# A one-core transformer layer step: another order for the last norm and the last gate, and other sources for some low halves of weights

## The chip, the core and the metric

The kernel runs on one core of one Trainium2 chip. A core has TensorE (matmuls; "PE" in the profile, "PEld" its weight loads), VectorE (DVE), ScalarE (ACT), GpSimd (POOL) and SyncE (SP), which here only issues transfers. Each engine works off its own queue in order. The metric is the device time of one execution in microseconds; three runs of the kernel before gave a median of 2521.23 us (2519.8 to 2523.84).

## The reference

One layer is applied to 2048 prompt tokens (empty states) and to 64 tokens of a second sequence (given states), with a model width of 1024:

```python
h = rms_norm(x, g_pre)
vA, bA, cA, zA, q, f, iv, zB, gA, gB = split_cols(h @ w_in)            # ten blocks of 1024 columns
u = cA * vA
yA = (silu(zA) * bA * causal_conv3(u_ext, conv_w)) @ w_a_out
fg = lb + (1 - lb) * sigmoid(f); logf = log(fg); kk = 1 - fg; qq = silu(q) * QK_SCALE
S_new, o = hgrn2_scan(S0, qq, kk, iv, logf)                            # 8 heads, chunks of 64 tokens
o = o * rsqrt(mean(o * o) + EPS) * g_onorm
yB = (o * silu(zB)) @ w_b_out
out = (sigmoid(gA) * yA + sigmoid(gB) * yB) @ w_o
x = x + rms_norm(out, g_post)
gate = sigmoid(rms_norm(x, g_ple) @ w_ple_gate)                        # "the last gate"
x = x + (p @ w_ple_proj) * gate
```

Results are x for both sequences and the new convolution and scan states.

## The kernel before, in words

**Number format.** Everything is float32. TensorE gets each weight and each operand as two parts: the high half, a cast that ScalarE writes, and the low half, the raw value minus the high half, a subtraction of VectorE. Both stand on line L230 (`split`). Each product takes three matmuls: high by high, high by low, low by high.

**Columns.** The 2112 tokens are worked off in three blocks of 768, 704 and 640 columns, features on the partitions. A block has two halves; a matmul of the last block has 320 columns. Temporaries (`r`) come from a ring of 48 tiles, half tiles (`hf`) from 8. Weights lie in `raw` (5 buffers), `hi` (4), `lo` (4) and `s` (3).

**Products.** Input projections come in groups of two output blocks (`sgroup`, matmuls on L457 to L459): seven products in place of eight, with sums S1 to S4 of weight blocks, sums T1 to T4 of operand blocks and the weight blocks A11, A12 and A22 themselves. Each product takes one 256 KB weight tile. The output projections (W_A, W_B, W_O) and the last block's W_G, which is the last gate, are done "in turn" (`in_turn`, L608 to L610): product 1 for all four pairs of output blocks, then product 2, and so on. The operand of the next product (for instance T2 = B22 - B12, line L562, and its split) is prepared while the present one runs, one tile after each pair.

**Low halves of weights.** `split_w` either makes a low half with the subtraction on VectorE or loads it from DRAM (`lows`), where block 1 left it: one more transfer of 256 KB on SyncE's queue, no work for VectorE, and a cast on L279 instead of L230 for the high half. Which way a sum goes is decided in `kept_w` by the list `fresh`: sums whose name stands there are subtracted anew. One list holds for the whole program; whoever reads it gets what was last written:

```python
return split_w(load_raw(sums[i1][name]), None if name in fresh else (i1, name), name in fresh)
```

In the last block `fresh` is empty for the gates and for `path_b`, holds S1 and S2 in `path_a`, and is cleared behind it. A12 and A22 of the input projections are always subtracted.

**Stages.** For each block: the gates gA and gB (8 groups; for the second and third block seven of them, `LEAD`, run right after the W_O of the block ahead, and the eighth inside `path_a`, when `side` calls `next(fills)` at j == 2), `path_b` (8 heads; per head one group for f and iv and one for zB and q), `path_a` (8 times two groups), W_A, W_B, W_O, and the norms. The attention of a head is hung between the matmuls of the next head's groups by hooks: scores on L1110, p_u on L1142, p_o on L1180 and L1182, the norm over a head's outputs with its power on GpSimd (L700 and L702) and the scaling on L1199. VectorE's gating of the keys and queries (L978 to L1038) stands between the splits of the same queue.

**End.** After the last block's W_O: its `final_norm` (squares of the eight output tiles on L741, added on L742; TensorE's transposes for the sum over features on L722; power on L702; scaling by g_post on L1446, + x on L1447; second squares; second root; scaling by g_ple on L1469). It is spread over the hooks of the `final_gate` of the block ahead, whose inputs wait in DRAM ("held": loaded by `asked`, split by `held_parts`), and of `ple`, the product p @ w_ple_proj. Then the last gate runs in turn; its `sink` applies the sigmoid (L1518), multiplies (L1520), adds x (L1521) and stores. Tables of numbers in `spread_out` say how many steps of each plan run at each hook.

Of the kernel before, what the change touches and what calls it, by code (L numbers as in the profile page):

```python
# [20 lines left out]
KB = D // P  # L21
# [73 lines left out]
def hybrid_step(  # L95
# [476 lines left out]

    def in_turn(stages, operand):

# [11 lines left out]

        for k in range(2):
            prepare(1, k)
        for i, (st, n) in enumerate(todo):
# [4 lines left out]
            for g in range(KH):  # L594
# [33 lines left out]
                elif what in ("p5", "p7"):  # L628
# [4 lines left out]
                    st["sink"](g, 1, 1, u2, p57)  # L633
                if i > 0:
                    prepare(i + 1, g)
                elif g < KH - 2:
                    prepare(1, g + 2)
# [240 lines left out]
    def gates(bl, hc, kept, first):  # L878


        groups = [(kind, j) for kind in (GA, GB) for j in range(0, KB, 2)]
        for kind, j in groups[: -1 if first else None]:
            outs = [rt(), rt()]
            n = groups.index((kind, j))
            sgroup(kind * 8 + j, kind * 8 + j + 1, hc, gate_sink(outs), first, by_k=n == 0 and not first, anew=n < LEAD)
            keep_gates(kept, kind, j, outs)
            yield
# [531 lines left out]

    def final_norm(bl, xo, acc, kept, take, early):  # L1420

        segs = bl["segs"]
        acc2, xks = None, []

        def fetch():
# [4 lines left out]

        for j in range(KB):
            sum_squares(j, xo[j], acc, width[0])
            if j % 2:
                yield
# [7 lines left out]
        for j in range(KB):  # L1444
            fetch()
            V.scalar_tensor_tensor(xo[j], xo[j], g_post[:, j : j + 1], rs, ALU.mult, ALU.mult)  # L1446
            V.tensor_tensor(xo[j], xo[j], xks[j], ALU.add)  # L1447
            if j == 0:
                acc2 = rt()
            sum_squares(j, xo[j], acc2, width[0])  # L1450
            yield
        stored = iter(range(0 if bl["last"] else KB))

        def store(n):
            for i in islice(stored, n):
                kept["x", i] = spill("x", i)
                paced(G.dma_start(kept["x", i], xo[i]))

        rs2 = rt()
# [35 lines left out]
    def final_gate(bl, h2, kept, by_k=False):  # L1495

        segs = bl["segs"]
        for j in range(KB):
            if by_k and j < 2:
                both = gemm_by_k([W_G, W_G + 1], h2, segs, (1,)) if j == 0 else both  # L1500
                pss = both[j]
            else:
                pss = gemm(W_G + j, h2, segs, (1,) if by_k else ())
            xj, pj, t = reload(kept["x", j]), reload(kept["p", j]), rt()
            for s, ps in zip(segs, pss):
                A.activation(t[:, cols_of(s)], ps, AF.Sigmoid)
            V.tensor_tensor(t, pj, t, ALU.mult)
            V.tensor_tensor(t, t, xj, ALU.add)
            G.dma_start(y_fm[j * P : (j + 1) * P, bl["t0"] : bl["t0"] + bl["n"]], t)
            yield  # L1510

    def gate_in_turn(bl, h2, xs, kept):


        def sink(g, c, h, x, y):
            j, s = g + c * KH, whole(x, y)
            t = hf() if y is None else s
            A.activation(t, s, AF.Sigmoid)  # L1518
            v = half(kept["p", j], h)
            (G if c == h == 0 else V).tensor_tensor(v, v, t, ALU.mult)  # L1520
# [149 lines left out]
    for bi, bl in enumerate(blocks):  # L1670
# [78 lines left out]
        for idx, n in in_turn(stages, a_first):  # L1749
# [3 lines left out]
            elif nxt and (idx, n) == (W_B, 6):  # L1753
                spread_out((next_ops(), (0, 1, 0, 1, 0, 1, 0) * KH))
            elif bl["last"] and idx == W_O and 1 <= n <= 4:
                run(asked, 2)
            elif bl["last"] and (idx, n) == (W_O, 5):
                a_first.clear()
                norm = sized(bl, final_norm(bl, xo, rt(), kept, lambda j, t: h2.append(t), 0))
                spread_out(  # L1760
                    (held_parts, (1,) * 4 + (2, 2)),
                    (norm, (0,) * 4 + (1,) * 4 + (2, 1, 0, 1, 1, 1, 2, 1, 2, 1, 1, 0) + (1, 1, 2, 1, 2, 1, 1)),
                    (sized(bl, ask_p()), (0,) * 16 + (1, 0, 0, 1)),
                    (sized(bl, first_halves()), (0,) * 24 + (1,) * 4),
                )
        if nxt:
            xo.extend(stages[-1]["mid"])
            fills = sized(nxt, gates(nxt, hc, kepts[bi + 1], False))
            norm = sized(bl, final_norm(bl, xo, rt(), kept, partial(split_h, h2) if first else partial(keep_h, kept), int(first)))
            spread_out((norm, (1,) * 6 + (0,) * 5 + (1, 0, 0, 1, 1) + (0, 1) * (KB - 1) + (0, 0, 1, 0, 0, 1) + (1, 0) * (KB - 3) + (1, 1, 1)))  # L1770
# [7 lines left out]
        else:  # L1778
# [55 lines left out]
```

## Time and profile before

| | us |
|---|---|
| median of three runs | 2521.23 |
| the profiled execution | 2522.08 |
| its span | 2520.4 |
| TensorE busy in it | 2495.2 (99%) |
| VectorE busy | 1943.3 (77%) |
| ScalarE busy | 1504.2 (60%) |
| GpSimd busy | 530.9 (21%) |
| DMA, mean over the span | 294 GB/s |

The stages that the change touches lie in the profiled execution about here: the seven groups of the last block's gates at 1690 to 1776 us, its `path_b` up to 2016, its `path_a` with the eighth gate group up to 2224, W_A, W_B and W_O up to 2374, the `final_gate` of the second block up to 2444, `ple` up to 2459, the last gate up to 2514, and the last stores up to 2520. A row of the profile's groups reads: line, engine, operation, output<-input, shapes, count | busy us, mean ns of one | idle time of the engine just before, and who ended most of it. A row of a table of windows reads: the stretch, its length, then for each engine the busy time with the instructions in brackets, then TensorE's granted clock, the share of the DMA engines' time, and GB/s.

### The profile page before, as it was taken

How to read it: one execution, taken by the hardware profiler on the slowest of the kernel's cores; microseconds unless marked ns; L12 is line 12 of the kernel's file. 1: busy time of each engine (PE TensorE's matmuls, PEld its weight loads, DVE VectorE, ACT ScalarE, POOL GpSimd, SP SyncE). 2: the span in 40 equal slices, each digit the busy share in tenths (PEclk: the TensorE clock that was granted, in tenths of full speed). 3: DMA queues.
4: the chain of work that ended last, by engine and by line, in shares of the span. 5: the costliest groups of instructions: out<-in, count | busy, mean ns of one | idle time of the engine just before them, and what ended most of it. 6: DMA issues, size and time to landing. Idle time of an engine off the chain costs nothing. (4 is left out here: it accounts for less than half of the span.)

```text
span 2520.4 us, 47301 instructions
## 1 busy us (share of the span) xinstructions
PE 2495.2 (99%) x16254; PEld 2476.1 (98%) x16254; DVE 1943.3 (77%) x3699; ACT 1504.2 (60%) x2926; POOL 530.9 (21%) x891
## 2 busy tenths in 40 slices
PE   9999999999999999999999999999999999999998
PEld 9999999999999999999999999999999999999998
DVE  7889999988867775588885667977677776679667
ACT  6676676554554763566555555676666655566645
POOL 2032222320022021122223221002122222110133
PEclk9999999999999999999999999999999999999999
DMA  8789889997687798788889988989988879888876
GB/s 330 241 305 338 313 297 324 330 318 266 231 334 263 258 330 292 255 272 284 280 282 332 336 299 310 323 272 355 329 285 290 276 260 324 279 304 307 292 250 212
DMA packets 341937, 741.95 MB, mean 294 GB/s; under 512 B 43062, under 2 KB 48240, under 8 KB 341696
## 3 DMA queue, kind: packets, MB, share of 16 engines
q1 hardware_dynamic: 284832, 515.76, 59.1%
q0 software_dynamic: 56864, 223.16, 24.8%
q8 instruction: 128, 2.10, 0.3%
q14 instruction: 113, 0.93, 0.1%
HBM read 526.40 MB, written 212.36 MB: 293 GB/s over the span
## 5 line engine op out<-in xcount | busy, mean ns | idle before, releaser
L457 PE MATMUL pg<-r,hi 128*128 128x320 f32 (+2 forms) x3304 | 1074.7, 325 | 1.7 <-DVE r L505 1.7
L458 PE MATMUL pg<-r,hi 128*128 128x320 f32 (+2 forms) x3304 | 1066.8, 323 | 0.0
L459 PE MATMUL pg<-r,lo 128*128 128x384 f32 (+2 forms) x2380 | 775.3, 326 | 0.0
L457 PEld LDWEIGHTS pg<-r,hi 128*128 128x128 f32 x3304 | 621.0, 188 | 4.0 <-DVE r L505 2.2
L458 PEld LDWEIGHTS pg<-r,hi 128*128 128x128 f32 x3304 | 621.6, 188 | 0.0
L279 ACT CAST hi<-raw 128x512 fp32r<-128x512 f32 x550 | 339.9, 620 | 407.7 <-PE pg L458 158.8
L459 PEld LDWEIGHTS pg<-r,lo 128*128 128x128 f32 x2380 | 447.1, 188 | 0.3 <-DMA lo<-low 0.3
L230 ACT CAST hi<-raw 128x512 fp32r<-128x512 f32 x420 | 259.4, 621 | 219.8 <-PE pg L458 81.0
L609 PE MATMUL pg<-r,hi 128*128 128x320 f32 (+2 forms) x976 | 313.3, 322 | 1.6 <-DVE r L230 1.5
L608 PE MATMUL pg<-r,hi 128*128 128x320 f32 (+2 forms) x976 | 310.4, 321 | 1.4 <-ACT r L230 1.4
L459 PE MATMUL pg<-r,s 128*128 128x352 f32 (+1 forms) x924 | 291.5, 315 | 2.1 <-DMA s<-low 2.1
L230 DVE TENSOR_TENSOR lo<-raw,hi 128x512 fp32r<-128x512 f32 x320 | 219.4, 687 | 93.5 <-ACT hi L230 88.6
L230 DVE TENSOR_TENSOR r<-r,r 128x320 fp32r<-128x320 f32 (+7 forms) x374 | 221.0, 611 | 44.1 <-ACT r L230 43.3
L230 ACT CAST r<-r 128x320 fp32r<-128x320 f32 (+7 forms) x374 | 195.9, 557 | 34.1 <-DVE r L1353 8.8
L610 PE MATMUL pg<-r,lo 128*128 128x320 f32 (+2 forms) x656 | 209.2, 319 | 0.0
L609 PEld LDWEIGHTS pg<-r,hi 128*128 128x128 f32 x976 | 183.9, 189 | 4.1 <-DVE r L230 3.8
L608 PEld LDWEIGHTS pg<-r,hi 128*128 128x128 f32 x976 | 182.9, 188 | 3.3 <-ACT r L230 2.9
L230 ACT CAST hi<-s 128x512 fp32r<-128x512 f32 x164 | 101.9, 623 | 126.9 <-PE pg L458 99.0
L459 PEld LDWEIGHTS pg<-r,s 128*128 128x128 f32 x924 | 173.5, 188 | 2.4 <-DMA s<-low 2.4
L471 ACT COPY hf<-pg 128x352 f32<-128x352 f32 (+2 forms) x354 | 157.5, 448 | 0.8 <-PE pg L459 0.7
L230 DVE TENSOR_TENSOR lo<-s,hi 128x512 fp32r<-128x512 f32 x164 | 114.1, 696 | 45.0 <-ACT hi L230 40.6
L505 DVE TENSOR_TENSOR r<-hf,pg 128x128 f32<-128x128 f32 (+5 forms) x164 | 64.3, 411 | 95.7 <-PE pg L459 95.4
(391 smaller groups left out, 4239.0 us busy)
## 6 DMA issues: line engine op xcount, KB each, us to landing
raw<-w_blk SPq DMA_DIRECT2D x559, 256.0 KB, 4.5
raw<-S SPq DMA_DIRECT2D x452, 256.0 KB, 4.1
lo<-low SPq DMA_DIRECT2D x332, 256.0 KB, 4.3
s<-low SPq DMA_DIRECT2D x218, 256.0 KB, 4.9
low<-lo SPq DMA_DIRECT2D x207, 256.0 KB, 4.0
S<-s SPq DMA_DIRECT2D x152, 256.0 KB, 4.1
low<-r POOLq DMA_DIRECT2D x66, 256.0 KB, 4.4
r<-w_blk POOLq DMA_DIRECT2D x64, 256.0 KB, 6.6
```

What stands on the lines that cost most here:

```text
L230: return A.copy(hi, src).ins, V.tensor_tensor(lo, src, hi.bitcast(F32), ALU.subtract).ins
L279: A.copy(hi, raw)
L457: add(hi[:, k, :], xhi, start=start and k == 0, stop=False)
L458: add(hi[:, k, :], xlo, start=False, stop=False)
L459: last[0] = add(lo[:, k, :], xhi, start=False, stop=k == KH - 1).ins
L471: copied = A.copy(got[n], ps[bank])
L505: V.tensor_tensor(dst, x, y, ALU.add)
L608: add(hi[:, k, :], xhi, start=start and k == 0, stop=False)
L609: add(hi[:, k, :], xlo, start=False, stop=False)
L610: last[0] = add(lo[:, k, :], xhi, start=False, stop=k == KH - 1).ins
```

## The change

It has six parts.

1. In the gates of the last block, `fresh` is set to S1 to S4 for groups n = 5 and n = 6 and to nothing for other n. It is written only there and, as before, ahead of and behind `path_a`. So it still holds S1 to S4 in all 16 groups of the last block's `path_b`; and it is emptied at j == 2 of `path_a`, where the eighth gate group runs.
2. End phase: the squares of output tiles 4 to 7 go first (before: 0 to 7 in order), and the norm's plan begins one product of W_O earlier. The transposes of the first sum (L722) come two hooks, that is one output block of `final_gate`, earlier, and so does the scaling by g_post. The loads of the held tiles begin one product earlier.
3. The last gate's operands are prepared two products ahead (`lead=2`).
4. The second weight halves of `final_gate` (8 tiles) and A11 and A12 of the last gate (8 tiles) have their low halves loaded.
5. In `final_gate` of the second block the + x (L1508) is done by GpSimd instead of VectorE. In the last gate's sink GpSimd does the multiplications of the first column half, VectorE those of the second; before, GpSimd did only those of output half 0, column half 0.
6. At the end of the second block the stores of x for later (8 of 360 KB on GpSimd's queue) are issued at the scaling of each tile instead of after all of them.

```diff
-    def in_turn(stages, operand):
+    def in_turn(stages, operand, lead=1):
...
-        for k in range(2):
+        for k in range(2 if lead == 1 else KH):
             prepare(1, k)
...
-                if i > 0:
-                    prepare(i + 1, g)
+                if lead > 1 or i > 0:
+                    prepare(i + lead, g)
                 elif g < KH - 2:
                     prepare(1, g + 2)
                 hook()
...
             n = groups.index((kind, j))
+            fresh[:] = ("S1", "S2", "S3", "S4") if bl["last"] and LEAD - 2 <= n < LEAD else ()
             sgroup(kind * 8 + j, kind * 8 + j + 1, hc, gate_sink(outs), first, by_k=n == 0 and not first, anew=n < LEAD)
...
-    def final_norm(bl, xo, acc, kept, take, early):
+    def final_norm(bl, xo, kept, take, early):
...
-        for j in range(KB):
-            sum_squares(j, xo[j], acc, width[0])
-            if j % 2:
+        acc = rt()
+        for i in range(KB):
+            sum_squares(i, xo[(i + KH) % KB if bl["last"] else i], acc, width[0])
+            if i % 2:
                 yield
...
             sum_squares(j, xo[j], acc2, width[0])
+            if not early:
+                store(1)
             yield
...
-                both = gemm_by_k([W_G, W_G + 1], h2, segs, (1,)) if j == 0 else both
+                both = gemm_by_k([W_G, W_G + 1], h2, segs) if j == 0 else both
...
-                pss = gemm(W_G + j, h2, segs, (1,) if by_k else ())
+                pss = gemm(W_G + j, h2, segs)
...
-            V.tensor_tensor(t, t, xj, ALU.add)
+            (G if by_k else V).tensor_tensor(t, t, xj, ALU.add)
...
-            (G if c == h == 0 else V).tensor_tensor(v, v, t, ALU.mult)
+            (V if h else G).tensor_tensor(v, v, t, ALU.mult)
...
-        return dict(idx=W_G, order=IN_TURN, raw=h2, anew=("A11", "A12"), sink=sink)
+        return dict(idx=W_G, order=IN_TURN, raw=h2, anew=(), sink=sink)
...
-            elif bl["last"] and idx == W_O and 1 <= n <= 4:
+            elif bl["last"] and idx == W_O and n < 4:
                 run(asked, 2)
-            elif bl["last"] and (idx, n) == (W_O, 5):
+            elif bl["last"] and (idx, n) == (W_O, 4):
...
-            for idx, n in in_turn([gate_in_turn(bl, h2, xo, kept)], a_first):
+            for idx, n in in_turn([gate_in_turn(bl, h2, xo, kept)], a_first, 2):
```

The built program has 1948 transfers on SyncE's queue instead of 1980: 8 fewer for the two gate groups, 64 fewer in `path_b`, 24 more in `path_a`, 16 more in the end phase.

**VectorE in a head of the last block's `path_b`.** Before, this stretch of its queue runs from the power's first step (L700) through the scaling of the heads' outputs (L1199) to the multiplication on L1026, whose result the scores' matmuls on L1110 read. `raw`, `hi`, `lo`, `s` are the tiles of a weight, `pg` and `pa` banks of matmul results:

```order
L700 TENSOR_SCALAR ms_23895<-ms_23895 128x1
L505 TENSOR_TENSOR r_23739<-hf_23796,hf_23811 128x320
L1199 TENSOR_TENSOR r_23885<-pa_23876,ms_23886 128x512
L1199 TENSOR_TENSOR r_23885<-pa_23892,ms_23895 128x128
L1038 SCALAR_TENSOR_TENSOR r_23740<-pg_23783,vec,r_23740 128x320
L505 TENSOR_TENSOR r_23739<-hf_23796,pg_23798 128x320
L1065 STREAM_TRANSPOSE r_23332<-r_23885 128x5x4x32
L498 TENSOR_TENSOR hf_23942<-hf_23796,pg_23830 128x320
L1025 SCALAR_TENSOR_TENSOR r_23739<-r_23739,r_23949 128x640
L1038 SCALAR_TENSOR_TENSOR r_23740<-hf_23942,vec,r_23740 128x320
L230 TENSOR_TENSOR lo_23990<-raw_23987,hi_23989 128x512
L1026 TENSOR_TENSOR r_23739<-r_23739,r_23727 128x640
```

After (the line numbers are 1 higher here):

```order
L230 TENSOR_TENSOR s_23984<-raw_23981,hi_23983 128x512
L1200 TENSOR_TENSOR r_23885<-pa_23892,ms_23895 128x128
L486 TENSOR_TENSOR hf_23811<-hf_23811,hf_23843 128x320
L498 TENSOR_TENSOR hf_23942<-hf_23796,pg_23830 128x320
L230 TENSOR_TENSOR lo_23990<-raw_23987,hi_23989 128x512
L505 TENSOR_TENSOR r_23739<-hf_23796,hf_23811 128x320
L1039 SCALAR_TENSOR_TENSOR r_23740<-hf_23942,vec,r_23740 128x320
L230 TENSOR_TENSOR s_23996<-raw_23993,hi_23995 128x512
L1066 STREAM_TRANSPOSE r_23332<-r_23885 128x5x4x32
L1026 SCALAR_TENSOR_TENSOR r_23739<-r_23739,r_23949 128x640
L230 TENSOR_TENSOR lo_24002<-raw_23999,hi_24001 128x512
L1027 TENSOR_TENSOR r_23739<-r_23739,r_23727 128x640
```

In a whole head twelve splits of weights (L230) stand on VectorE instead of four, and six more of them stand ahead of L1026 (now L1027).

**VectorE at the last gate's operands.** `hf_31582` and `hf_31613` are T2 for the first two pairs of tiles, made on L562 and then split. Before:

```order
L230 TENSOR_TENSOR lo_31654<-raw_31651,hi_31653 128x512
L562 TENSOR_TENSOR hf_31582<-r_31373,r_31296 128x320
L566 TENSOR_TENSOR r_31373<-r_31373,hf_31582 128x320
L230 TENSOR_TENSOR r_31586<-hf_31582,r_31586 128x320
L562 TENSOR_TENSOR hf_31613<-r_31375,r_31321 128x320
```

After (`hf_31496` is the first T2; L1472 is the scaling by g_ple, L1469 before):

```order
L230 TENSOR_TENSOR r_31375<-r_31296,r_31375 128x320
L559 TENSOR_TENSOR r_31296<-r_31296 128x320
L1472 SCALAR_TENSOR_TENSOR r_31429<-r_28390,vec,r_31191 128x640
L230 TENSOR_TENSOR r_31403<-r_31321,r_31403 128x320
L562 TENSOR_TENSOR hf_31496<-r_31373,r_31296 128x320
L564 TENSOR_TENSOR r_31296<-r_31373,r_31296 128x320
L230 TENSOR_TENSOR r_31431<-r_31346,r_31431 128x320
L1472 SCALAR_TENSOR_TENSOR r_31457<-r_28391,vec,r_31191 128x640
```

The first T2 now stands among the scalings of the norm (L1472) instead of behind them; the tiles of product 2 (B21, the five splits that stand between its L564 and L566 in the queue) and T2 are taken in turn with them.

More of the change, by code (lines that the diff above doesn't have):

```diff
@@ L1418, in out_in_turn, with store @@
         return stage
-    def final_norm(bl, xo, acc, kept, take, early):
+    def final_norm(bl, xo, kept, take, early):
         segs = bl["segs"]
         acc2, xks = None, []
+        stored = iter(range(0 if bl["last"] else KB))
+        def store(n):
+            for i in islice(stored, n):
+                kept["x", i] = spill("x", i)
+                paced(G.dma_start(kept["x", i], xo[i]))
         def fetch():
@@ L1450, in final_norm @@
             sum_squares(j, xo[j], acc2, width[0])
+            if not early:
+                store(1)
             yield
[L1452 to L1457, printed above, removed]
         rs2 = rt()
@@ L1754, in hybrid_step @@
                 spread_out((next_ops(), (0, 1, 0, 1, 0, 1, 0) * KH))
-            elif bl["last"] and idx == W_O and 1 <= n <= 4:
+            elif bl["last"] and idx == W_O and n < 4:
                 run(asked, 2)
-            elif bl["last"] and (idx, n) == (W_O, 5):
+            elif bl["last"] and (idx, n) == (W_O, 4):
                 a_first.clear()
-                norm = sized(bl, final_norm(bl, xo, rt(), kept, lambda j, t: h2.append(t), 0))
+                norm = sized(bl, final_norm(bl, xo, kept, lambda j, t: h2.append(t), 0))
                 spread_out(
[L1761 to L1764, printed above, removed]
+                    (held_parts, (0, 1, 0, 1) + (1,) * 6),
+                    (norm, (0,) * 4 + (0, 0, 1, 1) + (1, 3, 0, 1) + (0, 1, 1, 1, 2, 1, 1, 1, 1, 0, 1, 0) + (1, 1, 1, 2, 1, 1, 1, 1)),
+                    (sized(bl, ask_p()), (0,) * 14 + (1,) + (0,) * 6 + (1,)),
+                    (sized(bl, first_halves()), (0,) * 28 + (1,) * 4),
                 )
@@ L1768, in hybrid_step @@
             fills = sized(nxt, gates(nxt, hc, kepts[bi + 1], False))
-            norm = sized(bl, final_norm(bl, xo, rt(), kept, partial(split_h, h2) if first else partial(keep_h, kept), int(first)))
+            norm = sized(bl, final_norm(bl, xo, kept, partial(split_h, h2) if first else partial(keep_h, kept), int(first)))
             spread_out((norm, (1,) * 6 + (0,) * 5 + (1, 0, 0, 1, 1) + (0, 1) * (KB - 1) + (0, 0, 1, 0, 0, 1) + (1, 0) * (KB - 3) + (1, 1, 1)))
```

## Prediction
> **What bounds the kernel now.** I read the busy times first, then TensorE's waits, then windows over the places that wait, and only then single instructions.
>
> ```profile
> span 2520.4 us, 47301 instructions
> PE 2495.2 (99%) x16254; PEld 2476.1 (98%) x16254; DVE 1943.3 (77%) x3699; ACT 1504.2 (60%) x2926; POOL 530.9 (21%) x891
> ...
> PE pa L722 <- DVE r L742: 3.6, 1, 3.6
> PE pg L459 <- DMA s<-low: 2.1, 1, 2.1
> PE pg L609 <- DVE r L230: 1.5, 3, 0.9
> PE pg L608 <- ACT r L230: 1.4, 2, 0.9
> PE pa L1182 <- DVE r L1157: 1.2, 6, 0.3
> PE pa L1180 <- DVE r L1157: 0.8, 5, 0.2
> PE pa L1110 <- DVE r L1026: 0.5, 1, 0.5
> ```
>
> TensorE is busy for 99% of the span (waits: total us, times, longest). No matmul is removed, so whatever is gained must come from its waits. The last matmul starts here, so 2520.4 - 2513.8 = 6.6 us of tail follow:
>
> ```profile
> 2513.52 0.31 PE L610 MATMUL pg<-r,lo 128*128 128x320 f32 x1
> ```
>
> Two of the waits cost more than they last:
>
> ```profile
> 2434.54:2437.95 3.41, 0.07 (x1) 0.10 (x2) 2.36 (x3) 1.81 (x4) 2.46 (x5) 1.00 1.00 312
> 2437.95:2441.36 3.41, 3.41 (x14) 3.41 (x15) 2.49 (x4) 1.24 (x3) 0.00 (x0) 0.50 0.92 347
> 2475.50:2478.91 3.41, 1.55 (x7) 1.03 (x7) 3.38 (x5) 1.64 (x5) 2.94 (x5) 1.00 0.64 241
> 2478.91:2482.32 3.41, 3.35 (x12) 3.35 (x13) 2.96 (x7) 1.84 (x4) 1.31 (x2) 0.50 0.42 128
> 1768.94:1772.35 3.41, 2.37 (x17) 2.11 (x15) 2.61 (x4) 1.26 (x2) 0.42 (x1) 1.00 1.03 403
> 1772.35:1775.76 3.41, 2.31 (x16) 2.31 (x17) 0.00 (x0) 0.08 (x1) 1.18 (x3) 1.00 1.05 410
> ```
>
> After a stretch of 3.41 us with TensorE busy for 0.07, and after one with 1.55, the next ran at a granted clock of 0.50, which loses half of 3.41 us, 1.7 us, each time. After stretches with 2.37 and 2.31 busy it stayed at 1.00.
>
> **The change part by part.** *Lows of the gates and of `path_b`.* The 2.1 us of L459 lie in gate group n = 6, whose four sum lows are now subtracted: -2.1 us (0 to -2.1; the stores of x move into the same stretch, whose DMA share is 1.03 to 1.05 above). The list is not reset afterwards, so `path_b` of the last block also subtracts S1 to S4: per head eight loads fewer and eight subtractions more on VectorE. One head:
>
> ```profile
> 1880.96:1911.13 30.17, 29.81 (x230) 29.17 (x229) 23.42 (x53) 19.48 (x35) 7.58 (x12) 1.00 0.83 285
> ...
> L978 DVE TENSOR_SCALAR r<-r,lbt 128x640 f32<-128x640 f32 x1 | 0.6, 616 | 2.8 <-ACT r L976 2.8
> L1199 DVE TENSOR_TENSOR r<-pa,ms 128x512 f32<-128x512 f32 x1 | 0.7, 692 | 0.9 <-POOL ms L702 0.9
> L505 DVE TENSOR_TENSOR r<-hf,pg 128x128 f32<-128x128 f32 x2 | 0.5, 284 | 2.2 <-PE pg L459 2.2
> ...
> 1893.45 0.85 DVE L1026 TENSOR_TENSOR r<-r,r 128x640 f32<-128x640 f32 x1
> ...
> 1895.52 0.27 PE L1110 MATMUL pa<-r,r 128*64 128x64 f32 x1
> ...
> 1907.48 0.67 DVE L230 TENSOR_TENSOR lo<-raw,hi 128x512 fp32r<-128x512 f32 x1
> 1908.07 0.69 DVE L230 TENSOR_TENSOR s<-raw,hi 128x512 fp32r<-128x512 f32 x1
> ```
>
> VectorE works 23.42 of 30.17 us. Two splits follow each other at a pitch of 0.60 (1908.07 - 1907.48), so eight add 4.8: 28.2 us, still under the period. But its queue is in order, and three waits stand in it. The wait for TensorE (2.2) goes, because VectorE comes later. Of L978's 2.8 one more split fits in, leaving 2.2. L1199's 0.9 stays, and I add 0.5 for its second piece, whose power now stands behind the first scaling. 28.2 + 2.2 + 0.9 + 0.5 = 31.8, so 1.6 us beyond the period. The other way round: L1026 ends at 1894.30 and the scores' matmuls start at 1895.52, a slack of 1.2 us; six more splits ahead of it make 3.6, so 2.4 late in the first head. Behind L1026 stand the splits of the next products, for which TensorE then waits, and TensorE's results are in turn what L505 waits for, so that lateness is carried into the next head; in TensorE's own queue L1110 stands five matmuls later, which gives back 0.6 (29.81 us for 230). Between 1.6 and 2.4 I take 2.2 per head, 18 us for eight, nearer to the count along the chain. Bounds: nothing if all waits shrink as VectorE comes later (28.2 < 30.17); all waits kept, 28.2 + 5.9 + 0.5 = 34.6, so 4.4 per head, 35 us. That VectorE may be full without a loss is shown here (100% for 12 us, 91% for 200 us in the first block, TensorE full in both), but not with this chain of waits:
>
> ```profile
> 200.00:400.00 200.00, 200.00 (x1303) 198.72 (x1302) 182.74 (x338) 138.79 (x286) 56.02 (x80) 1.00 0.89 320
> ...
> 1725.50:1737.60 12.10, 12.10 (x85) 12.10 (x84) 12.10 (x19) 8.66 (x17) 1.07 (x2) 1.00 0.90 328
> ```
>
> *`path_a`.* From j = 2 on S1 and S2 are loaded, 24 loads of 256 KB (6.3 MB) more in 146 us, 43 GB/s:
>
> ```profile
> 2077.00:2223.00 146.00, 146.00 (x996) 146.00 (x995) 100.06 (x178) 80.75 (x156) 28.59 (x57) 1.00 0.85 294
> 1761.90:1776.20 14.30, 12.16 (x84) 11.90 (x83) 5.56 (x9) 5.25 (x10) 3.22 (x6) 1.00 1.04 409
> ```
>
> 294 + 43 = 337 GB/s lies under the 409 that one stretch moved, where however a load was 2.1 late. I take +1, half a wait (0 to +4, two such waits); the 24 splits that VectorE loses give time that nobody waits for (TensorE is full here).
>
> *First norm sooner.* The wait on L722 (3.6) and the slow clock behind it (1.7) hang on this chain:
>
> ```profile
> 2407.65 0.83 ACT L1506 ACTIVATE r<-pg 128x352 f32<-128x352 f32 x2
> 2416.07 0.80 ACT L1506 ACTIVATE r<-pg 128x352 f32<-128x352 f32 x2
> ...
> 2428.42 0.89 DVE L1508 TENSOR_TENSOR r<-r,r 128x704 f32<-128x704 f32 x1
> ...
> 2436.91 0.83 DVE L742 TENSOR_TENSOR r<-r,r 128x640 f32<-128x640 f32 x1 [0.80 <-ACT r L741]
> ...
> 2467.70 0.48 DVE L562 TENSOR_TENSOR hf<-r,r 128x320 f32<-128x320 f32 x1
> 2469.06 0.87 POOL L1520 TENSOR_TENSOR r<-r,hf 128x320 f32<-128x320 f32 x1 [21.17 <-ACT hf L1518]
> 2470.20 1.17 DVE L562 TENSOR_TENSOR hf<-r,r 128x320 f32<-128x320 f32 x1
> ```
>
> L742 at 2436.91 is the last addition of the second squares. The scaling ahead of it starts one output block sooner, 2416.07 - 2407.65 = 8.4 us. In the three and a half output blocks from there to L742 VectorE also loses four or five splits of weights (0.68 each, -3) and, with one ahead and one behind, five additions of x (0.89 each, -4.5). Against it GpSimd adds x: 704 columns at 0.87 for 320 make 1.9 us, an estimate, and if each held up VectorE for its whole length, five would cost 9.5. 8.4 + 3 + 4.5 - 9.5 = 6.4, more than the 3.6 needed. So the wait and its slow clock go: -5.3 (0 if more than six additions stand in the way, below; it can't gain more than the wait). What is late next is the reload of x for the last blocks on GpSimd's queue, behind whose additions the stores of y now also wait; nobody reads those. A page makes the row at 2470.20 a rule. The Trainium skill ("SBUF — State Buffer", the section "SBUF: two separate sides") says that a VectorE instruction with two SBUF inputs and a GpSimd instruction that reads SBUF take turns, each holding the port for its whole length. The trace agrees: L562 took 1.17 beside GpSimd's multiplication and 0.48 alone. By the rule the 9.5 is the price itself and not its ceiling, the sum stays as it is, and the GpSimd rival below gets its chance from it.
>
> *Operands of the last gate.* The waits from 2365 us on are these, beside L722:
>
> ```profile
> PE pg L608 <- ACT r L230: 1.4, 2, 0.9
> PE pg L609 <- DVE r L230: 1.3, 2, 0.9
> ...
> 2400.00:2425.00 25.00, 25.00 (x160) 24.97 (x159) 15.73 (x23) 10.00 (x19) 8.95 (x15) 1.00 0.69 232
> 2425.00:2450.00 25.00, 21.41 (x131) 21.13 (x130) 19.58 (x28) 9.71 (x22) 6.83 (x11) 0.93 0.83 291
> ```
>
> The 1.4 and 1.3 are T2's, made one product ahead, and they leave the stretch with only 1.55 us busy. One product for four pairs is 48 matmuls, by `path_a`'s 146.00 us for 996 about 7 us; two ahead leaves 14. So -2.7, and -1.7 for the clock: -4.4. It can't be more; it is 0 if the work only moves forward: the operands of B21, all prepared ahead of product 1 now, and T2 stand in VectorE's queue among the scalings by g_ple, and the last gate's first operands could be late instead. Those are split earlier (`first_halves`), so I keep -4.4. The second root's spread comes one hook later, 1.7 us, inside `ple`, which does not read it. Sixteen low halves more (4.2 MB in some 90 us, 47 GB/s) come on SyncE's queue where 232 to 291 GB/s move, under the 409 above: nothing; if that cover fails, one late load is 2.1.
>
> *Tail.* The last sink's additions stay; GpSimd has four multiplications of 0.87 more and may be in the way: +0.5 (-0.5 to +1.5).
>
> **Sum.** 18 - 2.1 + 1 - 5.3 - 4.4 + 0.5 = +7.7. The profiled execution took 2522.08, 0.85 more than the median of the three runs (2521.23); against the median this is 2529.
>
> **The rivals.** *VectorE absorbs the splits.* If the waits for ScalarE and TensorE shrink as VectorE comes later, 28.2 + 1.4 fits into 30.17 and `path_b` costs nothing. Then the sum is 7.7 - 18 = -10.3: 2511, faster. For it speak the two rows of a full VectorE; against it the six splits ahead of L1026 with 1.2 us of slack. It decides below 1.3 us per head (10.3 / 8). *The slow clock in each head.* A wait of 2.2 leaves some 1.2 of 3.41 us busy if it falls in one stretch, under the 1.55 that was followed by 0.50, so up to 8 x 1.7 = 13.6 more: 2543; the stretches with 2.31 speak against it if the wait straddles two. The Trainium skill ("TensorE: Matmul & The Clock Gate", the section "Why this matters for your kernels") warns only of gaps over about 3 us; by that no head would lose the clock. The row with 1.55 us busy, where no single wait was over 0.9, says otherwise. *GpSimd's additions hold the norm up.* If eight, not five, of 1.9 us stand in the chain (15.2), 8.4 + 3 + 4.5 - 15.2 leaves 0.7 of the 3.6, and the wait and its clock stay: +5.3, 2534; it decides from (8.4 + 3 + 4.5 - 3.6) / 1.9 = 6.5 additions on. That VectorE has idle time between them speaks against it. *Loads bound `path_a`* as in the last gate group: 2.1 for each of up to six of its groups, +12: 2540.
>
> **How the numbers follow.** Chances: forecast 0.48, absorbed 0.22, slow clock 0.18, GpSimd 0.07, loads 0.05. With the forecast's own 1.6 to 3 us per head it gives 2524 to 2535. The range goes from 2511 (absorbed) to 2545 (slow clock, 2543, and 2 for the other terms). Within 0.2%, about what a measurement here can tell, is 2516.2 to 2526.3: from 0.6 to 1.9 us per head, some of the forecast and of the absorbed case, 0.18. Faster is most of the absorbed case, 0.20; slower the rest, 0.62.
>
> **What would show it.** Right: heads of the last `path_b` longer than 30.17 us by about 2, VectorE above 90% there, a wait of L1110 for L1026 (one line lower in the new program) in each head; no wait on L722, no T2 waits, no 0.50 after 2430 us. Wrong: heads of 30.2 us, or a granted clock of 0.50 in them; a wait for low halves in `path_a`; GpSimd's additions ahead of L722.

## The result

The changed kernel took 2533.06 us (median of six runs, 2530.13 to 2536.8), the kernel before beside it 2522.75 (2519.8 to 2523.84): a ratio of 1.0043, interval 1.003 to 1.0056, so about 11 us slower. The profiled execution took 2530.13 with a span of 2528.0, 7.6 us longer than the span before; it is one of the two fastest runs, so it shows some 3 us less than the median.

The profile page of the changed kernel, and its list of TensorE's waits (total us, times, longest):

```profile
span 2528.0 us, 47324 instructions
...
PE 2495.1 (99%) x16254; PEld 2476.4 (98%) x16254; DVE 1964.6 (78%) x3719; ACT 1504.6 (60%) x2926; POOL 547.3 (22%) x903
```

```profile
PE pa L1111 <- DVE r L1027: 6.2, 7, 1.0
PE pa L710 <- POOL cols L702: 5.5, 1, 5.5
PE pg L459 <- DMA lo<-low: 3.8, 2, 2.0
PE pa L1183 <- DVE r L1158: 2.4, 8, 0.4
PE pg L459 <- DMA s<-low: 1.4, 1, 1.4
PE pa L1314 <- ACT r L1321: 1.2, 1, 1.2
```

TensorE does the same work (2495.1 us busy, 2495.2 before). The waits on L722, L609 and L608 are gone; in their place the scores (L1111, L1110 before) wait in seven heads for L1027 (L1026 before), the spread of the second root (L710) waits 5.5 us for GpSimd, and three low halves come late. Where the 7.6 us between the two spans lie, counted from the first matmul of each stage in the two traces:

| stage | before, us | after, us | difference |
|---|---|---|---|
| all ahead of the last block's gates | 1680.3 | 1678.8 | -1.5 |
| its gates, `path_b`, `path_a` | 543.6 | 554.5 | +10.9 |
| W_A, W_B, W_O | 150.3 | 149.4 | -0.9 |
| `final_gate` | 69.8 | 64.4 | -5.4 |
| `ple` | 14.8 | 23.0 | +8.2 |
| last gate | 55.0 | 49.7 | -5.3 |
| behind the last matmul | 6.6 | 8.2 | +1.6 |

One correction to what stands ahead: the first matmul of these gates is at 1680.3 us and that of `path_b` at 1770.9 (84 matmuls per group, counted in the trace). The wait of 2.1 us at 1773 us is therefore in the first group of `path_b`, not in the gate group n = 6 where the prediction puts it.

**A head of `path_b`.** One head of the changed kernel in the table of windows, from one L1111 to the next; then the stretch of VectorE's queue from L979 to the end of L1027, VectorE's waits there, and the matmul that waits for it:

```profile
1867.33:1898.66 31.33, 29.88 (x228) 29.17 (x228) 28.14 (x62) 19.51 (x34) 7.83 (x12) 1.00 0.66 209
...
1877.34:1898.62 21.28, 19.87 (x138) 19.23 (x136) 20.57 (x45) 14.60 (x27) 5.93 (x9) 1.00 0.64 199
```

```profile
DVE r L979 <- ACT r L977: 2.2, 1, 2.2
DVE r L1200 <- POOL ms L702: 0.7, 1, 0.7
```

```profile
1898.66 0.27 PE L1111 MATMUL pa<-r,r 128*64 128x64 f32 x1 [0.97 <-DVE r L1027]
```

The same stretch before:

```profile
1875.30:1894.32 19.02, 18.66 (x133) 18.28 (x132) 17.26 (x38) 13.57 (x26) 5.52 (x8) 1.00 0.76 271
```

```profile
DVE r L1199 <- POOL ms L702: 0.9, 1, 0.9
DVE qc L995 <- ACT r L993: 0.5, 1, 0.5
DVE qc L996 <- ACT qc L992: 0.2, 1, 0.2
```

A head takes 31.33 us instead of 30.17. In the stretch VectorE is now busy for 20.57 of 21.28 us; six splits and one small instruction more (45 instead of 38) make it 2.4 us longer, 3.3 of work less 0.9 of idle time that shrank (the window before opens 0.1 us ahead of L978, which starts at 1875.40). L1110 started 20.1 us after L978 before and 21.3 after: the 1.2 us of slack took the first half of the 2.4, the rest is what each head is late. Ahead of L979 2.2 us of idle time remain, so it is this stretch that is nearly full, and not VectorE as a whole. The granted clock in the heads stayed at 1.00.

**The second root.** The transposes of the second sum on TensorE (view of one source line), and what follows them on VectorE, GpSimd and TensorE (timelines of the changed kernel):

```profile
L722 PE MATMUL pa<-ident,r x6: 272/272/273, 2442.6 to 2443.2; 128*128 128x128 f32 x6
```

```profile
2437.08 0.88 DVE L1510 TENSOR_TENSOR r<-r,r 128x704 f32<-128x704 f32 x1
2437.89 3.08 DVE L742 TENSOR_TENSOR r<-r,r 128x640 f32<-128x640 f32 x2
...
2449.63 0.89 DVE L1510 TENSOR_TENSOR r<-r,r 128x704 f32<-128x704 f32 x1 [6.40 <-DMA r<-p]
2450.44 1.02 DVE L723 TENSOR_REDUCE cols<-pa 128x3 f32<-128x384 f32 x2
```

```profile
2438.10 2.18 POOL L1511 TENSOR_TENSOR r<-r,r 128x704 f32<-128x704 f32 x1 [1.51 <-ACT r L230]
...
2441.68 0.55 POOL L1340 DMA_DIRECT2D r<-p  x1
2443.32 1.70 POOL L1511 TENSOR_TENSOR r<-r,r 128x704 f32<-128x704 f32 x1 [1.10 <-DVE r L1510]
...
2446.42 0.55 POOL L1340 DMA_DIRECT2D r<-p  x1
2450.61 1.66 POOL L1511 TENSOR_TENSOR r<-r,r 128x704 f32<-128x704 f32 x1 [3.64 <-DVE r L1510]
2452.57 0.56 POOL L1512 DMA_DIRECT2D y_fm<-r  x1 [0.30 <-POOL r L1511]
2453.15 1.35 POOL L702 TENSOR_TENSOR cols<-cols,mhalf 128x6 f32<-128x6 f32 x1
```

```profile
2454.56 1.54 PE L710 MATMUL pa<-ident,cols 128*128 128x128 f32 x6 [5.52 <-POOL cols L702]
```

The transposes end at 2443.5. The sum over them (L723) stands on VectorE's queue behind the multiplication L1510, which sat 6.4 us for a load of p. That load is issued by GpSimd, whose queue now holds the additions: the issue at 2441.68 stands behind the addition of 2438.10 and its store, and that addition had to wait for an earlier multiplication, L1510 at 2437.08, whose result it adds to (the row names ScalarE's L230 as the releaser; it ended 0.1 us after the multiplication). From issue to landing these loads took up to 7.9 us (the view of L1340 between 2430 and 2460 us):

```profile
DMA to landing us min/median/max: 3.8/6.9/7.9
```

2441.68 and 7.9 are 2449.6, where L1510 starts. Then the power (L702) stands behind one more addition. The stretch without a matmul is followed by 6.8 us at half the clock, from 2453.1 to 2460.0 in the trace:

```profile
2451.10:2454.50 3.40, 0.00 (x0) 0.00 (x0) 1.64 (x3) 0.00 (x0) 3.08 (x3) 0.80 0.95 360
2454.50:2457.90 3.40, 3.34 (x14) 3.34 (x15) 1.72 (x3) 1.01 (x3) 2.29 (x3) 0.50 0.10 39
2457.90:2461.30 3.40, 3.40 (x19) 3.40 (x18) 3.40 (x5) 1.43 (x4) 0.00 (x0) 0.70 0.45 167
```

At 0.50 and 0.70 the last two stretches lose 1.7 and 1.0 us. With the wait of 5.5 that makes 8.2, all that `ple` became longer by.

### The profile page after: what moved, and what is told of

It is laid out like the page before. It is cut to its first block, busy times and chain, and to the rows that moved or that the text cites. A ratio compares the mean times of both kernels' runs of the same rounds, so it can differ in the third digit from the quotient of the medians.

```text
span 2528.0 us, 47324 instructions
## 1 busy us (share of the span) xinstructions
PE 2495.1 (99%) x16254; PEld 2476.4 (98%) x16254; DVE 1964.6 (78%) x3719; ACT 1504.6 (60%) x2926; POOL 547.3 (22%) x903
## 4 chain that ended last, share of the span: by engine, by line
PE 88%; DVE 4%; issue 4%; DMA 2%; ACT 1%; POOL 1%; SPq 0%; POOLq 0%; DVEq 0%; ACTq 0%
PE pg L457 19%; PE pg L459 19%; PE pg L458 19%; PE pg L609 6%; PE pg L608 6%; PE pg L610 6%; PE pg L646 2%; PE pg L647 2%; PE pg L645 2%; PE pa L1111 1%; PE pa L1183 1%; PE pa L1181 1%; PE pa L1143 1%; DMA r<-x 1%; DVE lo L230 1%
## 5 line engine op out<-in xcount | busy, mean ns | idle before, releaser
L230 ACT CAST hi<-raw 128x512 fp32r<-128x512 f32 x452 | 278.9, 621 | 257.4 <-PE pg L458 132.0
L609 PE MATMUL pg<-r,hi 128*128 128x320 f32 (+2 forms) x976 | 312.1, 321 | 0.0
L608 PE MATMUL pg<-r,hi 128*128 128x320 f32 (+2 forms) x976 | 309.7, 320 | 0.0
L230 DVE TENSOR_TENSOR lo<-raw,hi 128x512 fp32r<-128x512 f32 x346 | 237.2, 687 | 79.9 <-ACT hi L230 76.2
L230 DVE TENSOR_TENSOR r<-r,r 128x320 fp32r<-128x320 f32 (+7 forms) x374 | 225.9, 624 | 53.3 <-ACT r L230 52.2
L230 ACT CAST r<-r 128x320 fp32r<-128x320 f32 (+7 forms) x374 | 195.8, 557 | 34.4 <-DVE r L1354 8.2
L609 PEld LDWEIGHTS pg<-r,hi 128*128 128x128 f32 x976 | 183.1, 188 | 1.6 <-DVE r L230 1.3
L608 PEld LDWEIGHTS pg<-r,hi 128*128 128x128 f32 x976 | 182.5, 188 | 1.3 <-ACT r L230 1.0
L230 ACT CAST hi<-s 128x512 fp32r<-128x512 f32 x164 | 102.0, 623 | 127.2 <-PE pg L458 97.4
L230 DVE TENSOR_TENSOR lo<-s,hi 128x512 fp32r<-128x512 f32 x164 | 114.2, 697 | 45.3 <-ACT hi L230 42.2
```

The lines of the kernel that those rows point to most:

```text
L230: return A.copy(hi, src).ins, V.tensor_tensor(lo, src, hi.bitcast(F32), ALU.subtract).ins
L608: add(hi[:, k, :], xhi, start=start and k == 0, stop=False)
L609: add(hi[:, k, :], xlo, start=False, stop=False)
```

## The experiments

Each was timed beside the kernel before on its chip (medians 2521.75, 2522.46 and 2522.47 us in the three sets). All but the two of the last section are the kernel before with a part of the change in it; "the end" below means parts 2 to 5 of the change.

### The list in `path_b`

```diff
+        fresh[:] = ("S1", "S2", "S3", "S4") if bl["last"] else ()
         path_b(bl, hc, first, kept, fills, hs if first else None, prepare_sums(ahead_of, pieces=True))
```

> Only the list in the last block's path_b: S1 to S4 subtracted there, all else as before. Theory 1 (the stretch of VectorE's queue from L978 to L1026 is full, so each head is late there): heads of 31.3 us instead of 30.17, a wait of about 1.0 us of L1110 for L1026 in seven heads, 8 to 10 us slower in all. Theory 2 (the lost time of the changed kernel comes mainly from transfers and from the end): under 3 us slower.

2531.14 us (2527.92 to 2537.71), ratio 1.0036 (1.0023 to 1.0048): 9 us slower. The waits and one head:

```profile
PE pa L1110 <- DVE r L1026: 6.2, 7, 1.0
```

```profile
1870.02:1901.37 31.35, 29.86 (x228) 29.15 (x228) 28.14 (x62) 19.50 (x34) 7.95 (x12) 1.00 0.67 207
```

The same head as in the changed kernel, within 0.02 us. So the list, read by `path_b` where it should have been empty, by itself makes most of the loss.

With three names instead of four:

```diff
+        fresh[:] = ("S1", "S2", "S3") if bl["last"] else ()
```

> As the run with four sums, but S4 is loaded: ten splits in a head instead of twelve, seven instead of nine ahead of L1026. Theory 1 (a stretch that is full, with a threshold): two splits of 0.60 less ahead of L1026 take 1.2 us from a lateness of 1.0, so the wait for L1026 goes and heads are at 30.2 to 30.4: 0 to 2 us slower than before. Rival (each subtraction that VectorE gets costs its share): three quarters of what four sums cost, 6 to 8 us slower.

2535.71 us (2532.64 to 2537.1), ratio 1.005 (1.0038 to 1.0062): 12.6 us slower than before, not less than with four sums but rather more. Neither expectation held. Its waits, and the stretch from L978 to the end of L1026:

```profile
PE pa L1110 <- DVE r L1026: 8.8, 8, 1.6
...
PE pa L1180 <- DVE r L1157: 3.4, 7, 0.5
```

```profile
1878.38:1899.86 21.48, 19.32 (x133) 18.57 (x132) 20.09 (x43) 14.57 (x27) 6.72 (x9) 1.00 0.65 214
```

In this head, with two splits fewer, the stretch is 0.2 us longer. It has 0.7 us more idle time, and L1026 itself took longer beside GpSimd (timelines of VectorE and GpSimd; in the changed kernel the same instruction took 0.82):

```profile
1898.63 1.22 DVE L1026 TENSOR_TENSOR r<-r,r 128x640 f32<-128x640 f32 x1
```

```profile
1898.14 1.03 POOL L1078 COPY r<-r 128x640 f32<-128x640 f32 x1
```

This agrees with the Trainium skill ("SBUF — State Buffer", the section "SBUF: two separate sides"): a VectorE instruction with two inputs in SBUF and a GpSimd instruction that reads SBUF take turns. Where L1026 starts first, it is the copy that takes longer, 1.15 us at 1898.04 in the changed kernel and 0.72 alone. And TensorE's order is another one. Runs of matmuls in the traces, g for those of the groups, the number behind the x how many in a row (with four sums, from the third head on):

```
before    ... g x84  L1110 x30  g x60  L1142 x10  g x24  L1180 ...
three     ... g x84  L1110 x30  g x60  L1142 x10  g x24  L1180 ...
four      ... g x83  L1110 x30  g x55  L1142 x10  g x24  L1180 ...
```

With four sums the scheduler put L1110 five matmuls later against the groups behind it, some 0.7 us, and with three it did not. The heads of the two traces tell the parts apart. From L1110 to the next L978 it is 10.75 us with three sums and 10.03 with four; the first two heads with four, where the place is still the old one, have 10.75 too. So the place is worth 0.7 us per head. L1026 met the copy in three of the eight heads with three sums: the heads that ended there took 32.25 us and the two that follow on them 31.84, so the copy is worth 0.4. In those without the copy the stretch is 21.1 us, 0.2 shorter than with four sums, which is all that two splits fewer gave; why more idle time came in their place was not tried. How late a head is depends on the order that comes out, not on the number of splits alone.

With four sums, and the multiplication behind L1026 (L1027 before) done twice, 0.96 us more for VectorE behind the stretch:

```diff
-            V.tensor_tensor(chunks(qx), chunks(qe), f.unsqueeze(2).to_broadcast([P, nch, CH]), ALU.mult)
+            for _ in range(2 if bl["last"] else 1):
+                V.tensor_tensor(chunks(qx), chunks(qe), f.unsqueeze(2).to_broadcast([P, nch, CH]), ALU.mult)
```

> As the run with four sums, and L1028 of the last block is done twice with the same result: 0.96 us more on VectorE in each head, behind L1026 and ahead of the wait on L978 (2.2 us idle). Theory 1 (only work between L978 and L1026 counts): the idle time ahead of L978 falls to about 1.2 and heads stay at 31.3: within 2 us of four sums alone. Rival (VectorE's total counts): 0.96 more per head, 7 to 8 us slower than four sums alone.

2532.43 us (2529.28 to 2537.7), ratio 1.004 (1.0028 to 1.0052): 1.3 us over four sums alone, where each head would have cost 0.96, 7 to 8 in all, if VectorE's total counted. Two heads, and VectorE's wait over both:

```profile
1866.88:1898.96 32.08, 29.57 (x225) 28.78 (x225) 29.07 (x63) 19.54 (x34) 9.89 (x12) 1.00 0.66 214
1898.96:1930.62 31.66, 30.33 (x231) 29.62 (x231) 28.87 (x63) 19.59 (x34) 7.15 (x11) 1.00 0.66 206
```

```profile
DVE r L978 <- ACT r L976: 3.1, 2, 2.2
```

The idle time ahead of L978 fell from 4.4 to 3.1 us in two heads. In the profile these two heads are 0.5 us longer on average, half of the added work, so it is not free; the 1.3 of the medians lies within the spread of the runs. That VectorE's total decides is ruled out; that work behind the stretch costs nothing is not shown.

### The list in `path_a`

```diff
             n = groups.index((kind, j))
+            if bl["last"] and n >= LEAD:
+                fresh.clear()
```

> Only the list in path_a: S1 and S2 loaded from j = 2 on, 24 loads more, all else as before. If the two waits of the changed kernel there (1.8 and 1.4 us for lo<-low and s<-low) come from these loads: 2 to 4 us slower, with one to three such waits. Rival (they come from transfers that path_b's lateness or freed queue moved into path_a): no wait there, 0 to 1 us.

2528.2 us (2523.88 to 2531.67), ratio 1.0021 (1.0013 to 1.003): 5.3 us (3.3 to 7.6) slower by the ratio, more than the 2 to 4 expected and much more than the rival's 0 to 1. The waits for low halves:

```profile
PE pg L459 <- DMA lo<-low: 2.5, 2, 1.4
...
PE pg L459 <- DMA s<-low: 1.4, 2, 1.2
```

Only one of these (1.4 us, at 2073 us) lies in `path_a`; the others are near 1773 us, as before. The profiled execution took 2525.02, the fourth fastest of eleven. That the slower ones have more such waits is likely but not seen, so it is shown that these loads cost time, and not how all of the 5.3 us comes about.

### Gates and stores

Groups n = 5 and 6 subtract, and the list is emptied ahead of `path_b`:

```diff
+            if bl["last"] and n < LEAD:
+                fresh[:] = ("S1", "S2", "S3", "S4") if n >= LEAD - 2 else ()
...
+        fresh.clear()
         path_b(bl, hc, first, kept, fills, hs if first else None, prepare_sums(ahead_of, pieces=True))
```

> Only gate groups n = 5 and n = 6 of the last block subtract their four sum lows, and the list is empty again ahead of path_b. Theory 1 (the 2.1 us wait on L459 there is for the eight transfers that go): no wait over 0.5 us on L459 between 1690 and 1790 us, 2 us faster. Rival (the stretch is full of transfers in any case, and the wait only moves to another weight): a wait of 1 to 2 us in another group, within 1 us of before.

2522.59 us (2517.39 to 2524.45), ratio 0.9999 (0.999 to 1.0009). The wait near 1773 us is gone from the profile, and no gain is measured: other waits were longer in that execution (4.3 us on L722 instead of 3.6, 1.2 on L645 instead of 0.5). The interval reaches from 2.5 us faster to 2.3 slower, so a gain of 2.1 is not excluded.

The stores of x alone, each at the scaling of its tile:

```diff
...
             sum_squares(j, xo[j], acc2, width[0])
+            if not early:
+                store(1)
             yield
```

> Only the eight stores of x at the end of the second block are issued at the scaling of each tile. If they cause the changed kernel's 2.0 us wait for lo<-low at 1731 us: such a wait in the gate groups ahead of 1750 us, 1 to 3 us slower. Rival (harmless, the wait at 1731 comes from elsewhere): within 1 us of before, L459 waits 2 us near 1773 as before.

2521.41 us (2518.99 to 2524.51), ratio 0.9999 (0.999 to 1.0009). The wait moved from 1773 us to 1731 (1.1 us there), and the time is the same. The four traces with these stores all have such a wait at 1731 to 1734 us and none near 1773; none of the other traces has it. So the changed kernel's wait at 1731 comes with these stores; it only changes place.

### The end phase

Parts 2 to 5 of the change without the list and without the stores of x:

> Only the end phase of the change (norm's order, operands two products ahead, 16 more lows from DRAM, GpSimd adds x); list and stores of x as before. Theory 1 (the end gains the waits on L722, L608 and L609 with their two stretches of slow clock, 9.7 us, and gives 5.5 + 1.7 back to the second root's spread on L710, and about 1 in the tail): 1 to 3 us faster than before. Rival (the wait on L710 came only from the other parts): no such wait, 9 us faster.

2518.42 us (2515.94 to 2521.25), ratio 0.9986 (0.9977 to 0.9996): 3.5 us faster (1 to 5.8). TensorE's waits from 2365 us on:

```profile
PE pa L710 <- POOL cols L702: 2.7, 1, 2.7
PE pg L645 <- ACT hi L279: 1.8, 1, 1.8
```

L722, L608 and L609 are gone, L710 is there without the rest of the change. The other wait, on L645, is for the cast of a weight's high half. That cast stands on ScalarE's queue behind squares (L741) that wait for VectorE's L1454 in the norm:

```profile
2426.11 0.74 ACT L741 ACTIVATE r<-r 128x640 f32<-128x640 f32 x1 [6.76 <-DVE r L1454]
```

With each of the two waits comes a stretch of 3.41 us at a clock of 0.50. Two runs ask why they are there. First, the end with the loads of x and p on SyncE's queue, the additions still on GpSimd:

```diff
-            xj, pj, t = reload(kept["x", j]), reload(kept["p", j]), rt()
+            q = SP if by_k else G
+            xj, pj, t = reload(kept["x", j], queue=q), reload(kept["p", j], queue=q), rt()
```

> As the end phase alone, but the loads of x and p for the final gate are issued by SyncE instead of GpSimd. Theory 1 (these loads stand on GpSimd's queue behind its additions, come late, hold VectorE's multiplication of the gate and, behind it in the queue, the sum for the second root): the wait on L710 is under 1 us, 6 to 8 us faster than the end phase alone. Rival (the additions themselves, beside VectorE and ahead of the power, make it late): the wait on L710 stays over 3 us.

2511.56 us (2511.13 to 2513.83), ratio 0.9962 (0.9949 to 0.9975), 6.9 us under the end alone. Behind 2017 us TensorE has no wait of 0.25 us or more; the longest in the whole execution is that near 1773 us:

```profile
PE pg L459 <- DMA s<-low: 2.6, 1, 2.6
```

The loads themselves are not quicker from SyncE: those of p land after 5.7 to 9.9 us, in the changed kernel after 5.0 to 8.2. It is their issue that came late: the load that L723 stands behind was issued 53.3 us after the first matmul of `final_gate`, in the changed kernel 59.0 us after it. An L1454 still takes 2.33 us beside an addition here (0.82 alone), and no wait on L645 follows.

Second, the loads stay on GpSimd and the additions go back to VectorE:

```diff
-            (G if by_k else V).tensor_tensor(t, t, xj, ALU.add)
+            V.tensor_tensor(t, t, xj, ALU.add)
```

> The end phase alone, with the + x of the final gate left on VectorE; the loads of x and p stay on GpSimd's queue, which then has no additions. Theory 1 (the loads were late behind the additions): wait on L710 under 1.5 us, 4 to 6 us faster than the end phase alone, 2512 to 2515 us. Rival (VectorE needs the relief): a wait of 1 us or more on L722 or on L710 for VectorE's work, no faster than the end phase alone.

2509.73 us (2507.97 to 2510.26), ratio 0.9953 (0.9938 to 0.9968): 12.7 us faster than before, 8.7 under the end alone, and the fastest kernel here. TensorE is full from 2425 to 2475 us, the end of `final_gate`, `ple` and half of the last gate (columns of the windows as before, TensorE first):

```profile
2425.00:2450.00 25.00, 25.00 (x170) 24.80 (x168) 17.32 (x28) 16.18 (x42) 4.12 (x6) 1.00 0.91 295
2450.00:2475.00 25.00, 25.00 (x171) 24.93 (x171) 22.46 (x41) 20.20 (x49) 9.92 (x12) 1.00 0.92 315
```

The two remove different things, the loads from the queue or the additions from it, and both remove the waits on L710 and L645. With the additions still on GpSimd they went too, so it was not the additions' own time but the loads behind them. That VectorE does the additions again, 0.89 us per output block, brings no wait on L722: the sooner start and the splits that became loads were enough without GpSimd's help; which of the two was needed was not separated.

Last, the end with loads on SyncE, but the last gate's operands one product ahead:

```diff
-            for idx, n in in_turn([gate_in_turn(bl, h2, xo, kept)], a_first, 2):
+            for idx, n in in_turn([gate_in_turn(bl, h2, xo, kept)], a_first):
```

> The end phase with loads on SyncE (2511.6 us), but the last gate's operands one product ahead as before the change. If preparing two ahead is worth what the waits and the slow clock were: waits of 2.7 us on L608 and L609 come back, with a stretch at a clock of 0.50, 4 to 5 us slower: 2515 to 2517. Rival (the sooner norm alone would have removed them): within 1.5 us of 2511.6.

2516.96 us (2513.68 to 2518.97), 5.4 over the same kernel with two ahead. The waits are back, and with them a slower clock:

```profile
PE pg L608 <- ACT r L230: 1.4, 2, 0.9
PE pg L609 <- DVE r L230: 1.3, 2, 0.9
```

```profile
2469.02:2472.43 3.41, 1.98 (x10) 1.46 (x11) 3.38 (x5) 1.54 (x4) 3.01 (x4) 1.00 0.53 188
2472.43:2475.84 3.41, 3.41 (x15) 3.41 (x14) 3.29 (x8) 2.65 (x7) 0.82 (x2) 0.50 0.62 186
```

No single wait there is over 0.9 us, and a stretch of 3.41 us at half speed follows all the same. The Trainium skill ("TensorE: Matmul & The Clock Gate", the section "Why this matters for your kernels") warns of gaps over about 3 us; here several short ones, which left 1.98 of the 3.41 us ahead of the drop of the clock busy, did the same. Busy time alone gives no sharp limit in these traces: in the changed kernel the 3.41 us from 1729.5 us on had 1.57 busy, with most of the wait at 1731 in them, and the clock stayed at 1.00.

### The parts together

The changed kernel with its list as two groups of gates need it (empty in `path_b`, S1 and S2 in all of `path_a`):

```diff
-            fresh[:] = ("S1", "S2", "S3", "S4") if bl["last"] and LEAD - 2 <= n < LEAD else ()
+            if bl["last"] and n < LEAD:
+                fresh[:] = ("S1", "S2", "S3", "S4") if n >= LEAD - 2 else ()
...
+        fresh.clear()
         path_b(bl, hc, first, kept, fills, hs if first else None, prepare_sums(ahead_of, pieces=True))
```

> The changed kernel with its list mended: groups n = 5 and n = 6 of the gates subtract their sums, the list is empty in path_b and holds S1 and S2 in all of path_a. If the list's leak carries the whole slowdown (9.1 us in path_b, 5.4 in path_a, each measured alone) and the end phase gains 3.5: 2516 to 2520 us, heads of 30.2 us, the wait of 2.5 to 5.5 us on L710 still there. Rival (the parts act on each other, or the stores of x cost): 2522 or more.

2519.1 us (2515.88 to 2521.65), ratio 0.9984 (0.9975 to 0.9994): 14 us under the changed kernel, and the same as the end alone; the wait on L710 is still there with 5.3 us. And with the final gate's loads of x and p on SyncE as well (the edit shown above):

> As the changed kernel with the list mended, and the final gate's loads of x and p on SyncE's queue. If the gains add up: 7 us under the run with the mended list alone, 2509 to 2512 us, no wait over 1 us on TensorE behind 1690 us but those of the start. Rival (gates and stores bring nothing): 2511 to 2513 us, as the end phase with these loads on SyncE alone.

2510.96 us (2510.29 to 2512.07), ratio 0.996 (0.9945 to 0.9975), the same as the end with these loads on SyncE. Gates and stores together bring nothing that can be measured here.

The parts add up: 9.1 for `path_b` and 5.3 for `path_a`, less 3.5 for the end, are 10.9; the changed kernel is 10.8 slower by its ratio. Each of the three is known to some 2 or 3 us, so that they agree to 0.1 is chance.

## Why the prediction was right, and where not

The forecast was 2529 with 2511 to 2545, slower; it came out at 2533.06. The direction and the cause, the list that is not reset, were right. That the number came so near is luck: `path_b` cost 9 us less than its term, the end phase gained 5.7 less than its terms, `path_a` cost 4.3 more, and the gates gave none of their 2.1.

- *`path_b`, +18.* It measured +9.1 (5.8 to 12.1), half. The mechanism was the one named: L1110 waits for L1026 in each head. The step that failed is the 2.2 us per head; the trace shows 1.2. Of the two ways to count it, the waits along the queue (28.14 busy, 2.2 ahead of L978 and 0.7 at L1200 are 31.0 of 31.33) were nearer. I had added 0.5 for a second power that cost nothing. By the chain I had counted the six splits at their full 3.6 us on the stretch, which became only 2.4 longer, 0.9 of it for idle time that shrank. The 0.6 for the later place of L1110 was right: 0.7 in the traces of three and four sums.
- *Gates, -2.1.* No gain is measured. The wait was in the group behind the one that I took it for. Without the gates' eight loads it does go (the run with the gates alone); the list in `path_b` alone left 1.0 and 0.5 us of it. In the changed kernel another of 2.0 us came at 1731 with the stores of x. Why the gates alone gain no time stays open.
- *`path_a`, +1.* 5.3 (3.3 to 7.6), mostly above the bound of 4. The step that failed is the comparison of mean rates: 337 GB/s under the 409 seen elsewhere says nothing of a load that is late for its own product. The changed kernel has two such waits there, 3.2 us, and the runs of this part alone spread over 8 us.
- *First norm, -5.3.* Right: the wait on L722 and its slow stretch went, and `final_gate` is 5.4 us shorter. The additions on GpSimd did slow this chain, by the mechanism named (two L742 took 3.08 us together beside the addition of 2438.10), but the chain was early enough all the same: the transposes of 2442.6 waited for nothing. One row was misread on the way: the 1.17 us of L562 at 2470.20 stood beside GpSimd's addition L1521 (2470.01 to 2471.03), not beside the multiplication, which ended at 2469.93. The rule that the row was to show is not touched by it.
- *What would be late next.* I named a reload behind GpSimd's additions as what would be late next and gave it no price. That was the costliest slip: p is read by L1510, and behind L1510 in VectorE's queue stood L723. It cost 5.5 us on L710 and 2.7 for the clock. The rival of GpSimd's additions had the right engine, and its 2534 is the nearest of all to 2533.06, but by luck: it had the wrong place and the wrong mechanism. It was not the port and not the number of additions in the chain, but the loads behind them on the queue.
- *Operands of the last gate, -4.4.* Right: 5.4 between two ahead and one ahead, by 2.7 us of waits and a slow stretch.
- *Tail, +0.5.* 1.6 in the profile, just beyond the bound of 1.5; what in the last sink made it was not tried.
- *The rivals.* VectorE did not absorb the splits (heads of 31.3). The clock in the heads stayed at 1.00: the waits of 1.0 and 0.35 us leave over 2 of 3.41 us busy. Loads did hold `path_a` up in part.

## What to carry to other kernels

On GpSimd's queue here a transfer waited for the arithmetic ahead of it. Before work is moved onto a queue, list the loads that stand behind it, who reads them, and what stands behind those readers; here 0.89 us of relief on VectorE per block cost 8.7 us in the end phase. When splits are added to an in-order queue, find the stretch between a result that comes from another engine and the one that another engine awaits, and compare its idle time and the slack behind it with the added work; the mean busy share (77% of VectorE) says little. A list that one stage sets and others read is part of the change: count the transfers of the built program stage by stage.

## What was not expected of the hardware

Ten splits per head cost no less than twelve, since the order that came out of the scheduler was another (0.7 us per head) and L1026 met a GpSimd copy in three of the heads (1.22 us instead of 0.82). And waits of at most 0.9 us each were enough for half the clock, with 1.55 us (the kernel before) and 1.98 us (the last gate one product ahead) busy of the 3.41 us ahead of the drop, while heads with waits of 1.0 and 0.35 us some 16 us apart kept it at 1.00.
